# Experts ranked by their tokens on the chip, four of them in 64 places and two passes, with a part of the weights' low parts on GpSimd

## The chip, the cores and the metric

One core of one Trainium2 chip. The metric is the device time of one execution in microseconds, as the median of the runs. Engines: PE (TensorE), DVE (VectorE), ACT (ScalarE), POOL (GpSimd), SP (SyncE, which issues the DMAs).

## What is computed

Two decoder layers over 256 tokens of width 1024, all in fp32. Each has a norm, four token mixers side by side, an output projection, a second norm and a channel mixer: a dense SwiGLU in the first layer, and in the second eight SwiGLU experts of width 3584, of which every token uses two. The part that the change speaks of:

```python
def moe_swiglu(h, router, wg, wu, wd):
    t = h.reshape(-1, D)
    logits = (t @ router).astype(jnp.float32)
    top_vals, top_idx = lax.top_k(logits, TOP_K)
    gates = jax.nn.softmax(top_vals, axis=-1)
    combine = jnp.sum(jax.nn.one_hot(top_idx, N_EXPERTS) * gates[..., None], axis=1)
    y = jnp.zeros(t.shape, jnp.float32)
    for e in range(N_EXPERTS):
        y = y + combine[:, e:e + 1] * swiglu(t, wg[e], wu[e], wd[e])
    return y
```

## The kernel before, in words

All large weights lie in one tensor as chunks of 128 x 2048 floats (1 MB). SP loads them in their order of use into buffers that are taken in turn: `RING` = 9 of them, and `RING2` = 8 more in the MoE stage, in the memory that the mixers have left.

TensorE takes fp32 operands in one pass only with a part of their digits. So every chunk is split, half by half (`halves`, L159 to L178): ACT writes the high part `hi` of 128 x 1024 (L170), DVE the low part `lo` = weight - hi (L171). There are `HALVES` = 4 pairs of such buffers. The other operand is split in the same way by `part` (L206, L207). A product is then three products (`moving`, L188): high by high, low of x by high, high of x by low part of the weights. In the mixers some halves name POOL for the low part (`on_pool`); in the MoE stage none does.

The MoE stage (`moe`) finds the two experts of each token, the place of each token in its expert (`pos`) and the weights (`comb`). `experts` goes through the eight experts in their order. For one of them up to 128 tokens are gathered with a one-hot product (`gather`), transposed and split (`gathered_T`), and stand in TensorE as the stationary operand of 128 columns; the weights move past it, 512 columns at a time. An expert has seven slabs of 512 hidden columns. A slab has six chunks, two each for gate, up and down projection: 24 products for each, 72 in all. `gate_or_up` makes the gate's sum, which ACT puts through silu (L977) into `xs`; DVE multiplies the up sum with it (L981); `act_T` transposes the result (L920), splits it into `hmh` and `hml`; `down` adds it to two banks, and runs one slab behind. At an expert's end `scatter` adds the rows back to `x` with their weights (L955, L956).

If an expert has more than 128 tokens, a second run through all eight takes the places from 128 on (L1000).

The order within each engine's queue is set by the scheduler of the language, not by hand, in the expert loop. Engines work their queues in order. SP's DMAs wait for a free buffer; the gain of the last norm (L125, loaded into `xs`) waits for the last use of `xs` by the last expert's transposes (L892).

The splitting that all stages share:

```python
            eng = nc.gpsimd if j in on_pool else nc.vector
            ...
                nc.scalar.activation(hi, w, AF.Copy)
                eng.tensor_tensor(out=lo, in0=w, in1=hi.bitcast(F32), op=SUB)
```

## Time and profile before

| | us |
|---|---|
| median of 3 runs | 1442.94 |
| lowest and highest | 1442.29 and 1443.75 |
| span of the profiled execution | 1440.7 |
| of it up to the first products of the experts | about 437 |
| PE busy, DVE busy, ACT busy, POOL busy | 1396.5, 1203.5, 981.2, 79.0 |

The times of the runs are those of whole executions. The page gives the profiled execution by its span alone, from the first instruction to the last, and this span is what sums are made against. A busy PE is not PE at its peak: the ends of products are modelled, so a product of 512 columns shows some 394 ns while the next one starts after 229. How far apart products start tells PE's pace.

### The profile page before, as it was taken

What the parts mean: (1) busy time and instruction counts of PE and PEld (TensorE: products, weight loads), DVE (VectorE), ACT (ScalarE), POOL (GpSimd) and SP (SyncE); (2) the same over time, 40 slices, a digit from 0 to 9 for tenths busy, and PEclk for the clock granted to TensorE, in tenths of its full rate; (3) what the DMA queues carried; (4) which work ended last, traced back from release to release, by engine and by line L of the source; (5) the groups of instructions that cost most, each with busy time, mean ns of one, the idle gap of its engine ahead of it and who ended that gap; (6) DMA issues with size and microseconds to landing.
All of it is one profiled execution on the core that took longest, in us unless ns stands there. A gap on an engine that the chain in (4) does not pass through costs nothing.

```text
span 1440.7 us, 19053 instructions
## 1 busy us (share of the span) xinstructions
PE 1396.5 (97%) x6993; PEld 1156.4 (80%) x6994; DVE 1203.5 (84%) x1495; ACT 981.2 (68%) x1223; POOL 79.0 (5%) x46
## 2 busy tenths in 40 slices
PE   8889999998899999999999999999999999999996
PEld 6678999996777888888888888888788888877885
DVE  6986555569968999999998988898898889889886
ACT  5464444453657878788787877777777777777774
POOL 3221000014130000000000000000000000000000
PEclk9999999999999999999999999999999999999998
DMA  9424555553387999999999899999999999919980
GB/s 371 162 111 175 202 181 187 188 211 111 114 353 285 364 373 349 363 370 346 347 362 356 332 362 360 342 368 366 343 350 369 353 350 352 370 67 369 421 333 32
DMA packets 59574, 422.12 MB, mean 293 GB/s; under 512 B 6608, under 2 KB 6864, under 8 KB 9168
## 3 DMA queue, kind: packets, MB, share of 16 engines
q1 hardware_dynamic: 59472, 420.82, 76.9%
q8 instruction: 57, 0.93, 0.3%
q14 instruction: 45, 0.37, 0.1%
HBM read 419.74 MB, written 1.05 MB: 292 GB/s over the span
## 4 chain that ended last, share of the span: by engine, by line
PE 72%; DVE 4%; ACT 1%; issue 0%; POOLq 0%; ACTq 0%; DVEq 0%
PE acc L199 45%; PE sc L199 21%; PE tr L920 2%; DVE cv L381 1%; PE tr L881 1%; DVE lo L171 1%; PE tr L955 1%; PE tr L892 0%; DVE xc L419 0%; ACT hi L170 0%; PE sc L449 0%; DVE raw L856 0%; DVE cv L379 0%; PE tr L243 0%; DVE sel L750 0%
## 5 line engine op out<-in xcount | busy, mean ns | idle before, releaser
L171 DVE TENSOR_TENSOR lo<-raw,hi 128x1024 fp32r<-128x1024 f32 x770 | 916.5, 1228 | 155.4 <-ACT hi L170 132.4
L170 ACT ACTIVATE hi<-raw 128x1024 fp32r<-128x1024 f32 x790 | 803.8, 1056 | 199.2 <-PE acc L199 109.5
L199 PE MATMUL acc<-lo,xgh 128*128 128x512 f32 x896 | 353.0, 394 | 0.7 <-DVE lo L171 0.3
L199 PE MATMUL acc<-hi,xgh 128*128 128x512 f32 x896 | 353.3, 394 | 0.1
L199 PE MATMUL acc<-hi,xgl 128*128 128x512 f32 x896 | 351.2, 392 | 0.0
L199 PEld LDWEIGHTS acc<-lo,xgh 128*128 128x128 f32 x896 | 168.3, 188 | 43.3 <-DVE lo L171 4.4
L199 PEld LDWEIGHTS acc<-hi,xgl 128*128 128x128 f32 x896 | 168.4, 188 | 36.2
L199 PEld LDWEIGHTS acc<-hi,xgh 128*128 128x128 f32 x896 | 168.4, 188 | 34.9 <-ACT xgh L206 0.4
L199 PE MATMUL sc<-hi,hmh 128*128 128x512 f32 x448 | 176.4, 394 | 0.0
L199 PE MATMUL sc<-hi,hml 128*128 128x512 f32 x448 | 175.4, 392 | 0.0
L199 PE MATMUL sc<-lo,hmh 128*128 128x512 f32 x448 | 161.8, 398 | 0.0
L199 PEld LDWEIGHTS sc<-hi,hml 128*128 128x128 f32 x448 | 84.2, 188 | 18.3
L199 PEld LDWEIGHTS sc<-hi,hmh 128*128 128x128 f32 x448 | 84.2, 188 | 18.1
L199 PEld LDWEIGHTS sc<-lo,hmh 128*128 128x128 f32 x448 | 81.9, 188 | 16.3
L199 PE MATMUL sc<-hTh,hi 128*128 128x256 f32 x336 | 93.0, 277 | 0.0
L199 PE MATMUL sc<-hTl,hi 128*128 128x256 f32 x336 | 92.8, 276 | 0.0
L199 PE MATMUL sc<-hTh,lo 128*128 128x256 f32 x336 | 92.8, 276 | 0.0
L206 ACT ACTIVATE hmh<-tr 128x512 fp32r<-128x512 f32 x56 | 33.4, 596 | 68.0 <-PE tr L920 68.0
L199 PE MATMUL acc<-lo,hTh 128*128 128x512 f32 (+1 forms) x192 | 69.4, 388 | 9.2 <-DVE lo L171 9.1
L199 PE MATMUL acc<-hi,hTh 128*128 128x512 f32 (+1 forms) x192 | 70.9, 397 | 0.2
L977 ACT ACTIVATE xs<-acc 128x512 f32<-128x512 f32 x56 | 33.2, 592 | 55.1 <-PE acc L199 55.1
L199 PE MATMUL acc<-hi,hTl 128*128 128x512 f32 (+1 forms) x192 | 70.6, 388 | 0.0
(234 smaller groups left out, 1394.8 us busy)
## 6 DMA issues: line engine op xcount, KB each, us to landing
raw<-wst SPq DMA_DIRECT2D x393, 1024.0 KB, 6.2
raw<-gains SPq DMA_DIRECT2D x4, 512.0 KB, 4.7
raw<-wst SPq DMA_DIRECT2D x4, 512.0 KB, 12.5
pl<-par_l SPq DMA_DIRECT2D x2, 803.5 KB, 9.1
out<-raw SPq DMA_DIRECT2D x4, 256.0 KB, 4.1
x<-x_in SPq DMA_DIRECT2D x2, 256.0 KB, 3.2
x<-x_in SPq DMA_DIRECT2D x1, 512.0 KB, 8.6
xs<-gains SPq DMA_DIRECT2D x1, 512.0 KB, 4.5
```

Of the source, the lines that this page charges most:

```text
L170: nc.scalar.activation(hi, w, AF.Copy)
L171: eng.tensor_tensor(out=lo, in0=w, in1=hi.bitcast(F32), op=SUB)
L199: nc.tensor.matmul(ps, lhs, rhs, start=start and all(m[0] is not ps for m in seq[:n]), stop=stop and all(m[0] is not ps for m in seq[n + 1:]))
L206: a = nc.scalar.activation(hi, src, AF.Copy)
L381: nc.vector.scalar_tensor_tensor(cv[:, ct], src, wk_, cv[:, ct], op0=MUL, op1=ADD)
L881: nc.tensor.matmul(pg[q].rearrange("p k c -> p (k c)"), OH[e][:, t], src[:, t, HF[q]], start=t + n == 0, stop=t + n == 2)
L920: nc.tensor.transpose(ps[:, n], hm[:, n * P:(n + 1) * P], ident)
L955: nc.tensor.matmul(ps, OT[e][:, t], y, start=n == 0, stop=n == 1)
L977: nc.scalar.activation(sg, pg, AF.Silu)
```

## The change

- **Ranking.** `ranks` counts the tokens of each expert and sorts experts 1 to 7 by their number on DVE. SP reads the ranks into registers (L1089 of the changed kernel), and the chunks of all experts but the first are loaded from addresses that depend on them. Expert 0 comes first, then the ranks in the order 3, 0, 4, 1, 5, 2, 6 (`TURNS`).
- **Narrow turns.** The ranks 3 to 6 get 64 places. The high part of their tokens stands in columns 0 to 63 of the stationary operand and the low part in columns 64 to 127 (`both`). Two products then do, with the high and the low part of the weights. The two halves of the rows of a gate's or up projection's sum have to be added: ACT or DVE copies the sum from PSUM to `two` (`folded`, L996 and L998), and one product with a shifted identity (`fold`, L1001) adds the lower rows to the upper ones. Expert 0 and ranks 0 to 2 stay as they are (wide turns).
- **POOL.** In a wide slab 2 of 12 low parts are POOL's, in a narrow one 3 of 12: the second half of the second chunk of gate, up and down projection (`POOLED`).
- **Buffers.** `RING` goes from 9 to 8, `HALVES` from 4 to 5.
- **The second run** is taken when an expert has more tokens than its places.

The comments are left out of the changed file, so lines move: L170, L171 become L182, L183; L977 becomes L1097; L981, L1100; L920, L1028; L199, L211.

```diff
-RING = 9
+RING = 8
-HALVES = 4
+HALVES = 5
+WIDE = 3
+TURNS = (3, 0, 4, 1, 5, 2, 6)
+NARROW = P // 2
+POOLED = ((((), (1,)), ((), (1,)), ((), (1,))), (((), (1,)), ((), ()), ((1,), ())))
...
+            def ranks():
...
+                nc.vector.tensor_add(key, num, cs[:, C_TIE:C_TIE + 8])
+                nc.vector.max(top, key)
+                nc.vector.max_index(ri, top, key)
...
+                def both(hi_lo, ps):
+                    hi = hi_lo[:, :, LO]
+                    nc.scalar.activation(hi, ps[:, :, LO], AF.Copy)
+                    nc.vector.tensor_tensor(out=hi_lo[:, :, UP], in0=ps[:, :, LO], in1=hi.bitcast(F32), op=SUB)
...
+                def rows(items, start, stop):
+                    if len(items[0][1]) == 2:
+                        products([moving(*it) for it in items], start, stop)
+                    else:
+                        products([[(ps, xx[0], w[n])] for n in range(2) for ps, xx, w in items], start, stop)
+                def folded(ps, which, then):
+                    cf = FT[which]
+                    if which == 0:
+                        nc.scalar.activation(cf, ps, AF.Copy)
+                    else:
+                        nc.vector.tensor_copy(cf, ps)
+                    def f():
+                        nc.tensor.matmul(ps, fold, cf, start=False, stop=True, skip_group_check=True)
+                        then()
+                    soon.append(f)
+                def catch_up():
+                    while soon:
+                        soon.pop(0)()
...
-                        hs = w0 if w0 and i + which + j == 0 else halves(c0 + ECH * e + 6 * s + 2 * which + j)
+                        hs = w0 if w0 and i + which + j == 0 else halves(
+                            turns[e].chunk(6 * s + 2 * which + j, False), POOLED[turns[e].wide][which][j])
...
+                        if j == 0:
+                            catch_up()
...
+                    for r in range(NE - 1):
+                        v = nc.values_load(rank_i[0:1, r:r + 1], engines=[mybir.EngineType.SP], min_val=0, max_val=NE - 1)
+                        ranked_c.append(v * ECH + MOE0)
+                    turns = turns + [Turn(ranked_c[r], pos_r, comb_r, r, r < WIDE) for r in TURNS]
...
                     pg = gate_or_up(i, 0)
-                    nc.scalar.activation(sg, pg, AF.Silu)
+                    if narrow:
+                        folded(pg, 0, lambda pg=pg: silu(pg))
+                    else:
+                        silu(pg)
```

How it moves instructions, at two places. ACT in one slab of the expert loop, from one eviction of the transposed activations to the next gate's silu, before. L170 writes high parts of the weights: four of the gate's (raw_8063, raw_8085), two of the up projection's (raw_8118); acc_8062 is the gate's sum.

```order
L206 ACTIVATE hmh_8113<-tr_8108 128x512
L170 ACTIVATE hi_8065<-raw_8063 128x1024
L170 ACTIVATE hi_8069<-raw_8063 128x1024
L170 ACTIVATE hi_8087<-raw_8085 128x1024
L170 ACTIVATE hi_8091<-raw_8085 128x1024
L170 ACTIVATE hi_8120<-raw_8118 128x1024
L170 ACTIVATE hi_8124<-raw_8118 128x1024
L977 ACTIVATE xs_81<-acc_8062 128x512
```

The same engine in a slab of a narrow turn of the changed kernel, from the up projection's first half on (raw_7739 and raw_7759 are its chunks, raw_7778 and raw_7798 the down projection's, acc_7692 the gate's sum):

```order
L182 ACTIVATE hi_7741<-raw_7739 128x1024
L996 ACTIVATE two_7417<-acc_7692 128x512
L182 ACTIVATE hi_7745<-raw_7739 128x1024
L1097 ACTIVATE xs_81<-acc_7692 128x512
L182 ACTIVATE hi_7761<-raw_7759 128x1024
L182 ACTIVATE hi_7765<-raw_7759 128x1024
L182 ACTIVATE hi_7780<-raw_7778 128x1024
L182 ACTIVATE hi_7784<-raw_7778 128x1024
L182 ACTIVATE hi_7800<-raw_7798 128x1024
L182 ACTIVATE hi_7804<-raw_7798 128x1024
L957 ACTIVATE hmh_7859<-tr_7854 128x4x64
L182 ACTIVATE hi_7819<-raw_7817 128x1024
```

The copy of the gate's sum (L996) is new and stands one high part ahead of where the silu stood, so that the up projection's later high parts come behind both.

DVE in one slab before, from the up projection's second half on (L981 multiplies; raw_8118 and raw_8140 are the up projection's chunks, raw_8163 and raw_8185 the down projection's):

```order
L171 TENSOR_TENSOR lo_8125<-raw_8118,hi_8124 128x1024
L171 TENSOR_TENSOR lo_8143<-raw_8140,hi_8142 128x1024
L171 TENSOR_TENSOR lo_8147<-raw_8140,hi_8146 128x1024
L171 TENSOR_TENSOR lo_8166<-raw_8163,hi_8165 128x1024
L981 TENSOR_TENSOR xs_81<-acc_8117,xs_81 128x512
L171 TENSOR_TENSOR lo_8170<-raw_8163,hi_8169 128x1024
L171 TENSOR_TENSOR lo_8188<-raw_8185,hi_8187 128x1024
L171 TENSOR_TENSOR lo_8192<-raw_8185,hi_8191 128x1024
L207 TENSOR_TENSOR hml_8259<-tr_8253,hmh_8258 128x512
```

And in a slab of a narrow turn of the changed kernel, one whole period (acc_7738 is the up projection's sum; raw_7817 and raw_7835 are the next gate's chunks):

```order
L183 TENSOR_TENSOR lo_7742<-raw_7739,hi_7741 128x1024
L183 TENSOR_TENSOR lo_7746<-raw_7739,hi_7745 128x1024
L183 TENSOR_TENSOR lo_7762<-raw_7759,hi_7761 128x1024
L998 CAST two_7417<-acc_7738 128x512
L183 TENSOR_TENSOR lo_7781<-raw_7778,hi_7780 128x1024
L183 TENSOR_TENSOR lo_7785<-raw_7778,hi_7784 128x1024
L1100 TENSOR_TENSOR xs_81<-acc_7738,xs_81 128x512
L183 TENSOR_TENSOR lo_7801<-raw_7798,hi_7800 128x1024
L958 TENSOR_TENSOR hmh_7859<-tr_7854,hmh_7859 128x4x64
L183 TENSOR_TENSOR lo_7820<-raw_7817,hi_7819 128x1024
L183 TENSOR_TENSOR lo_7824<-raw_7817,hi_7823 128x1024
L183 TENSOR_TENSOR lo_7838<-raw_7835,hi_7837 128x1024
```

The low parts of the second halves of raw_7759, raw_7798 and raw_7835 are gone from here; they stand in POOL's queue. The copy of the up sum (L998) comes right behind the first half of the chunk whose second half is POOL's, and two low parts stand between it and the multiplication.

## Rows read from the trace of the kernel before

**Rows 1.** the page, engines: busy us (share of the span) xinstructions

```profile
PE 1396.5 (97%) x6993; PEld 1156.4 (80%) x6994; DVE 1203.5 (84%) x1495; ACT 981.2 (68%) x1223; POOL 79.0 (5%) x46
```

**Rows 2.** windows: PE, PEld, DVE, ACT, POOL busy, PEclk, DMA share, GB/s

```profile
802.00:926.00 124.00, 123.90 (x559) 100.92 (x559) 110.75 (x109) 92.85 (x106) 0.00 (x0) 1.00 0.95 354
1310.00:1390.00 80.00, 78.90 (x353) 64.03 (x353) 71.31 (x69) 59.50 (x66) 0.00 (x0) 1.00 1.01 420
```

**Rows 3.** chain of waits: start us, us, engine, tile, line, xinstructions

```profile
554.95 5.51 PE sc L199 x24
1298.73 5.51 PE sc L199 x24
...
854.71 11.00 PE acc L199 x48
871.65 11.00 PE acc L199 x48
```

**Rows 4.** groups by line, 802 to 926 us: xcount | busy us, mean ns

```profile
L171 DVE TENSOR_TENSOR lo<-raw,hi 128x1024 fp32r<-128x1024 f32 x85 | 98.9, 1220 | 10.0 <-ACT hi L170 10.0
L170 ACT ACTIVATE hi<-raw 128x1024 fp32r<-128x1024 f32 x84 | 82.7, 1052 | 1.6 <-PE acc L199 1.2 <-DVE lo L171 0.3
L199 PE MATMUL acc<-lo,xgh 128*128 128x512 f32 x112 | 44.3, 396 | 0.1
L981 DVE TENSOR_TENSOR xs<-acc,xs 128x512 f32<-128x512 f32 x7 | 4.8, 692 | 3.2 <-PE acc L199 3.2
L920 PE MATMUL tr<-cs,xs 128*128 128x128 f32 x28 | 4.2, 272 | 0.0
L977 ACT ACTIVATE xs<-acc 128x512 f32<-128x512 f32 x7 | 4.2, 598 | 10.0 <-PE acc L199 10.0
L901 ACT ACTIVATE ot<-tr 128x256 fp32r<-128x256 f32 x1 | 0.4, 387 | 1.4 <-PE tr L899 1.4
```

**Rows 5.** timeline of ACT and DVE, one slab: start, us, [idle before]

```profile
860.24 0.60 ACT L977 ACTIVATE xs<-acc 128x512 f32<-128x512 f32 x1 [1.91 <-PE acc L199]
868.47 0.60 ACT L206 ACTIVATE hmh<-tr 128x512 fp32r<-128x512 f32 x1 [1.90 <-PE tr L920]
...
861.81 3.50 DVE L171 TENSOR_TENSOR lo<-raw,hi 128x1024 fp32r<-128x1024 f32 x3 [1.53 <-ACT hi L170]
```

**Rows 6.** timelines of POOL and DVE in the mixers

```profile
401.14 2.39 POOL L171 TENSOR_TENSOR lo<-raw,hi 128x1024 fp32r<-128x1024 f32 x1 [0.26 <-ACT hi L170]
...
401.83 0.48 DVE L617 SCALAR_TENSOR_TENSOR hTl<-tr,gd,hTh 128x256 fp32r<-128x256 f32 x1
402.22 2.38 DVE L171 TENSOR_TENSOR lo<-raw,hi 128x1024 fp32r<-128x1024 f32 x1
...
49.93 3.68 POOL L171 TENSOR_TENSOR lo<-raw,hi 128x1024 fp32r<-128x1024 f32 x1 [5.03 <-ACT hi L170]
...
50.14 1.22 DVE L171 TENSOR_TENSOR lo<-raw,hi 128x1024 fp32r<-128x1024 f32 x1
...
331.35 11.80 POOL L171 TENSOR_TENSOR lo<-raw,hi 128x1024 fp32r<-128x1024 f32 x2 [3.26 <-ACT hi L170]
...
338.26 2.62 DVE L381 SCALAR_TENSOR_TENSOR cv<-zp,pl,cv 128x256 f32<-128x256 f32 x1
```

**Rows 7.** L381 and L171 alone: xcount, min/median/max ns

```profile
L381 DVE SCALAR_TENSOR_TENSOR cv<-zp,pl,cv x120: 468/476/2665, 27.7 to 368.6; 128x256 f32<-128x256 f32 x120
...
L171 POOL TENSOR_TENSOR lo<-raw,hi x20: 2357/2414/9247, 10.5 to 427.6; 128x1024 fp32r<-128x1024 f32 x20
```

**Rows 8.** SP's waits: us in total, times, longest us

```profile
SPq L139 <- DVE lo L171: 919.4, 316, 22.7
SPq L125 <- PE tr L892: 36.2, 1, 36.2
```

**Rows 9.** L999 alone: duration ns min/median/max

```profile
L999 SPq TENSOR_LOAD <-cnti x1: 479/479/479, 1382.5 to 1382.5; - x1
```

**Rows 10.** window at the stage's start, columns as in rows 2

```profile
430.00:440.00 10.00, 7.55 (x32) 5.09 (x33) 7.99 (x29) 4.86 (x8) 0.00 (x0) 0.83 0.52 203
```

More of the change, by code (lines that the diff above doesn't have):

```diff
@@ L57 @@
 C_PLACE = C_IOTA + 8
-C_END = C_PLACE + P
+C_TIE = C_PLACE + P
+C_CAP = C_TIE + 8
+C_END = C_CAP + 8
 Q_RT = 0
@@ new lines, in ranked, with weights @@
+            def ranked(dst, src):
+                t_ = xs[:, 1, :NT * 64].rearrange("p (t r e) -> p t r e", t=NT, r=8)
+                for t in range(NT):
+                    nc.vector.tensor_mul(t_[:, t], by_rank, src[:, t].unsqueeze(1).to_broadcast([P, 8, 8]))
+                nc.vector.tensor_reduce(dst, t_, axis=AX.X, op=ADD)
+            ranks()
+            one_off.close()
+            wk = st.enter_context(tc.tile_pool(name="mw", bufs=1, reuse_waits="tile"))
+            def weights():
@@ L921, in act_T @@
                     hh = wk.tile([P, 4, P], F32R, name="hmh", bufs=2)
-                    hl = wk.tile([P, 4, P], F32R, name="hml", bufs=2)
-                    part(hh, hl, ps)
-                    HT[i] = (hh, hl)
+                    if turns[i // NSLAB].wide:
+                        hl = wk.tile([P, 4, P], F32R, name="hml", bufs=2)
+                        part(hh, hl, ps)
+                        HT[i] = (hh, hl)
+                    else:
+                        both(hh, ps)
+                        HT[i] = (hh,)
                 def down(i, between=()):
@@ L930, in down @@
                     for j in range(2):
-                        hs = halves(c0 + ECH * e + 6 * s + 4 + j)
+                        hs = halves(turns[e].chunk(6 * s + 4 + j, i == NE * NSLAB - 1 and j == 1), POOLED[turns[e].wide][2][j])
                         order = [(n, hf) for n in range(2) for hf in range(2)]
@@ L935, in down @@
                             order.sort(key=lambda o: o[1])
-                        products([moving(DP[e][hf], cut(HT[i], ALL, 2 * j + n), cut(hs[n], ALL, HF[hf])) for n, hf in order],
-                                 s + j == 0, s == NSLAB - 1 and j == 1)
+                        rows([(DP[e][hf], cut(HT[i], ALL, 2 * j + n), cut(hs[n], ALL, HF[hf])) for n, hf in order],
+                             s + j == 0, s == NSLAB - 1 and j == 1)
+                        if j == 0:
+                            catch_up()
                         for f in between if j == 0 else ():
@@ L971, in experts, with silu, mul @@
                 one_hot_T(0)
-                if place is pos:
+                if oh is not None:
                     weights()
+                    for r in range(NE - 1):
+                        v = nc.values_load(rank_i[0:1, r:r + 1], engines=[mybir.EngineType.SP], min_val=0, max_val=NE - 1)
+                        ranked_c.append(v * ECH + MOE0)
+                    turns = turns + [Turn(ranked_c[r], pos_r, comb_r, r, r < WIDE) for r in TURNS]
                 for i in range(NE * NSLAB):
                     e, s = divmod(i, NSLAB)
+                    narrow = not turns[e].wide
+                    def silu(pg):
+                        nc.scalar.activation(sg, pg, AF.Silu)
+                    def mul(pu):
+                        nc.vector.tensor_mul(hm, pu, sg)
                     pg = gate_or_up(i, 0)
-                    nc.scalar.activation(sg, pg, AF.Silu)
+                    if narrow:
+                        folded(pg, 0, lambda pg=pg: silu(pg))
+                    else:
+                        silu(pg)
                     if s:
@@ L980, in experts @@
                     pu = gate_or_up(i, 1)
-                    nc.vector.tensor_mul(hm, pu, sg)
+                    if narrow:
+                        folded(pu, 1, lambda pu=pu: mul(pu))
+                    else:
+                        mul(pu)
                     if s == NSLAB - 1 and e + 1 < NE:
                         gather(e + 1)
+                        catch_up()
                     if s:
@@ L995, in experts @@
                 finish(adds, raw().rearrange("p (t d) -> p t d", t=NT))
-            experts(pos, oh, w0)
-            most = nc.values_load(cnti[0:1, 0:1], min_val=0, max_val=S)
-            with tc.If(most > P):
+            ranked_c = []
+            experts([Turn(MOE0, pos, comb, 0, True)], oh, w0)
+            most = nc.values_load(cnti[0:1, 0:1], min_val=0, max_val=2 * S)
+            with tc.If(most > S):
                 pos2 = mo.tile([P, NT, 8], F32, name="pos2")
-                nc.vector.tensor_scalar(pos2, pos, float(P), None, op0=SUB)
-                experts(pos2)
+                off = mo.tile([P, 8], F32, name="off")
+                nc.vector.tensor_reduce(off, by_rank[:, WIDE:NE - 1].rearrange("p r e -> p e r"), axis=AX.X, op=ADD)
+                nc.vector.tensor_scalar(off, off, float(NARROW - P), float(P), op0=MUL, op1=ADD)
+                for t in range(NT):
+                    nc.vector.tensor_sub(pos2[:, t], pos[:, t], off)
+                experts([Turn(MOE0 + e * ECH, pos2, comb, e, True) for e in range(NE)])
     done = mixer(0, 0, None)
```

94 lines of the change are left out of this document (69 added, 25 removed).

## The prediction

> **What bounds the kernel now.** I first read the busy shares of the page: PE is busy for 97% of the span, DVE for 84%, POOL for 5% [rows 1]. Then the stretches: over the expert of 802 to 926 us PE is busy for 99.9% of the time at a granted clock of 1.00 (its level of 2.4 GHz), DVE for 89%, ACT for 75%, POOL not at all [rows 2]. The weights look like a second limit there, since the 16 DMA engines show a share of 0.95 at 354 GB/s; but from 1310 to 1390 us, where the queue catches up, the same engines move 420 GB/s [rows 2]. Six chunks of 1.049 MB, which is what a slab needs, take 15.0 us at that rate, and DMA is not the limit. The chain of waits shows the period. The first products of two experts lie at 554.95 and 1298.73 us, six experts apart: 124.0 us for an expert. Two slabs of one expert start at 854.71 and 871.65 us: 16.94 us for a slab, of which 48 products take 11.00 us, so 0.229 us each [rows 3]. Seven slabs make 118.6 us; the other 5.4 us are the change of expert (gather, transposes). So the MoE stage is PE's, eight times 124.0 us, and the other engines wait for it inside their queues: ACT stands idle for 1.91 us ahead of the silu (L977) and 1.90 us ahead of the eviction hmh, DVE for 1.53 us until a high part comes [rows 5].
>
> **The change, part by part.** All sums go against the profiled execution, 1440.7 us; the median of the runs lies 2.2 us above it.
>
> *Fewer passes.* Of the 504 weight products of a narrow expert 168 go and 14 folds come: 154 times 0.229 us is 35.3 us less of PE. It is a gain only if nothing else then needs more than 16.94 us for a slab. DMA needs 15.0 us. ACT has twelve high parts at 0.985 us (82.7 us by 84) and three smaller operations: 13.4 us [rows 4]. That would be about 2 us less than now in each of the 28 narrow slabs.
>
> *The ring of waits in a narrow slab.* The engines work their queues in order, and the new order closes a ring. ACT's first eviction of the gate (L996) waits for the gate's last product. After it stand one high part, the silu (L1097) and the two high parts of the up projection's second chunk; the low part of the last one is POOL's; PE must use it before DVE can copy the up result (L998); after that copy DVE has two low parts in front of the multiplication (L1100); then come four transposes and ACT's eviction (L957); and only behind this the four high parts of the next gate stand, the last of which has its low part on POOL again. Priced by rows [rows 4, 7]:
>
> - eviction 0.60, high part 0.985, silu 0.60, two high parts 0.985 + 1.05: 4.22 us
> - POOL's low part, 2.36 us, and PE's last two products, 0.23 + 0.39 = 0.62 us
> - DVE's copy, not in the trace, at the price of the other 512-column operations on PSUM, 0.69 us
> - two low parts at 1.164 us (98.9 by 85), the multiplication 0.69: 3.02 us
> - transposes 0.60 us, eviction of 256 elements 0.39 us
> - four high parts 4.00 us, POOL 2.36 us, PE 0.62 us
>
> The sum is 18.9 us, more than PE's 16.94. Priced the same way, the ring of before has neither copies nor POOL in it: silu, three high parts, a low part, the multiplication, transposes, eviction, four high parts, a low part and the last products make 12.6 us. It fits into 16.94, as the idle times of ACT say [rows 5].
>
> *POOL against DVE.* Nothing in the MoE stage of before shows them together, so I go by the mixers. At 401.14 us POOL starts a low part of 2.39 us; DVE's own low part, issued at 402.22, takes 2.38 us instead of 1.22 and ends 1.07 us behind POOL's. From 49.93 us POOL needs 3.68 us because it first waits for a low part of DVE that ends at 51.36. An L381 that takes 0.476 us in the median takes 2.62 us at 338.26, when POOL is in: 2.14 us lost [rows 6, 7]. Operations that read PSUM go on (L617, 0.48 us at 401.83 inside POOL's span). So a low part moved to POOL saves DVE 1.16 us and can cost it 2.14 us. In a narrow slab nine on DVE, three on POOL and the three operations on PSUM are 10.5 + 6.4 + 1.8 = 18.7 us: the pair is as full as the ring is long. Two of POOL's three low parts are in the ring already. The third, of the down projection's second chunk, becomes ready about 8 us into the ring, while DVE does the two low parts ahead of the multiplication. If it gets in between them, the ring grows by 2.14 us to 21.0; if DVE finishes first, it stays at 18.9.
>
> The rows show both orders: POOL got in behind a single low part at 51.36 us, and waited out a chain of L381 from 331.35 us on, where its two low parts took 11.80 us [rows 6]. The Trainium skill ("SBUF — State Buffer", Who interferes with whom) says that whichever of the two issues first holds the shared port for its whole instruction. By that rule POOL would always enter after one low part, and the slab would take 21.0 us; by the row at 331.35 it would take 18.9. The Trainium skill ("Perfetto Trace Analysis", GPSIMD Engine Instruction) calls GpSimd's spans in a profile unreliable; with the 2.14 us that DVE lost in place of POOL's 2.36, twice, the ring would be 0.4 us shorter.
>
> I take the middle, 20.0 us: 3.06 us more than now. 28 such slabs: +86 us (+55 to +114).
>
> *Change of expert in a narrow turn.* At 5.4 us it is PE's now; PE is idle for some 8 us of a 20 us slab and can do part of it there. I take half off, 4 times 2.7 us: -11 us (-22 to 0).
>
> *Wide turns.* 84 x 3 products as before. DVE and POOL need ten low parts, two of POOL's and two operations on PSUM, 11.6 + 4.3 + 1.4 = 17.3 us if nothing overlaps, against PE's 16.94. The operations on PSUM don't wait for POOL, so most of it fits: +4 us over 28 slabs (0 to +8).
>
> *Ranks.* Some sixteen DVE operations of 0.1 to 0.2 us and two for the fold stand among the first low parts, where PE waits: the stretch from 430 to 440 us already has PE at 7.55 of 10 us and a granted clock of 0.83 [rows 10]. +3 us (0 to +6). SP's seven register loads, at 0.48 us (L999) 3.4 us together, stand behind the twelve chunks that SP has issued ahead, some 34 us of PE's work at 2.8 us each: hidden [rows 9].
>
> *A buffer less.* SP waits 919 us in all for a buffer to come free [rows 8], so it runs as far ahead as buffers allow. Sixteen buffers are 45 us of PE's work instead of 48. The longest hold is the gain of the last norm, 36.2 us in which SP issues nothing else [rows 8]. It still fits: +1 us (0 to +3).
>
> *Sum:* 86 - 11 + 4 + 3 + 1 = +83, which is 1523.7 us for the execution and **1526 us** for the median. The bounds are 55 - 22 = +33 and 114 + 8 + 6 + 3 = +131: 1476 to 1574 us, the forecast's own range.
>
> **Rivals.**
>
> *The narrow slabs run at the speed of DMA.* The ring opens if ACT and POOL run ahead in the five pairs of buffers and POOL does not hold DVE up. Then a narrow slab takes 15.0 us, 28 x -1.94 = -54; with -11 and +8 from above the median is 1386 us. It decides from where a slab falls under 16.94 us. For it: PE, ACT and DMA each have the room. Against it: ACT's queue has the gate's eviction ahead of the up projection's high parts, and in every case of [rows 6] in which both engines read two SBUF operands one of the two stood still.
>
> *Only the port counts.* If the waits fill each other and just the serial work on the shared port is left, 9 x 1.164 + 3 x 2.14 = 16.9 us, a slab is what it was: 0 - 11 + 8 gives a median of 1440 us, no change within what can be told.
>
> *The clock falls.* With PE busy for 12 of 20 us, its level may drop to 1.2 GHz for a while, as it did between 430 and 440 us [rows 10]. PE's three steps in the ring, 0.62 + 0.60 + 0.62 us, would double: at most 28 x 1.84 = +51 us, a median of 1577 us.
>
> *The change falls back.* With more than 64 tokens for one of the last four experts the whole stage runs a second time, about +990 us. The reference's routing gives 62, 66, 94, 33, 86, 63, 56 and 52 tokens; the fourth of the ranked seven has 63, so it takes two flips by rounding.
>
> **How the numbers follow.** The forecast gets 0.62, DMA's speed 0.15, the port alone 0.12 (half of it over 0.2% faster, half within), the clock 0.10, the second pass 0.01. About 0.2% is what a measurement of this kernel can tell from no change. Faster is 0.15 + 0.06 = 0.21, within 0.06, slower 0.73. A range of 1425 to 1580 us takes in the forecast's own, the port alone and the clock, and leaves out DMA's speed, the second pass and a few tails, together 0.2.
>
> **What would show it.** In the changed profile: narrow slabs of 19 to 21 us beside wide ones of 17; low parts of DVE (L183) of over 2 us wherever one of POOL lies beside them; ACT idle ahead of L957 and L996, DVE ahead of L998; DMA's share well under 0.9 in the narrow turns. I am wrong if narrow slabs take under 17 us, if DVE's low parts stay at 1.22 us beside POOL, or if the wide slabs grow by over 0.5 us.

## The result, and the profile after

The changed kernel takes 1632.6 us (median of four runs, 1630.7 to 1635.2), the kernel before 1442.6 us on the same chip: a ratio of 1.132, with an interval of 1.130 to 1.134. Slower was right; 83 us were forecast and 190 came, well outside the range. The profiled execution spans 1633.7 us against 1440.7, so 193.0 us have to be found.

The page of the changed kernel, engines, as in [rows 1]:

```profile
PE 1402.1 (86%) x6378; PEld 1047.7 (64%) x6378; DVE 1229.8 (75%) x1402; ACT 969.7 (59%) x1251; POOL 441.1 (27%) x186
```

PE has 615 instructions fewer and is busy for longer; no engine but PE is above 75%. The windows, columns as in [rows 2], of a wide turn, a narrow turn, one wide slab and one narrow slab:

```profile
732.00:868.00 136.00, 130.51 (x561) 99.93 (x560) 113.34 (x97) 92.92 (x107) 38.09 (x14) 1.00 0.88 328
868.00:1032.00 164.00, 122.33 (x406) 75.80 (x406) 114.78 (x94) 92.26 (x111) 52.77 (x21) 0.91 0.74 267
802.40:821.10 18.70, 18.20 (x80) 13.87 (x79) 15.55 (x13) 12.96 (x16) 4.98 (x2) 1.00 0.91 338
908.10:931.40 23.30, 16.72 (x55) 10.05 (x54) 16.25 (x12) 12.83 (x16) 7.58 (x3) 0.93 0.72 268
```

A narrow slab takes 23.3 us, a wide one 18.7, both 16.94 before. In neither does an engine work for the whole time, and DMA's share falls to 0.74. In the narrow turn the mean granted clock is 0.91. From the starts of the silu, which mark the slabs, the 193.0 us come out as follows: the first silu at 461.3 us instead of 446.6, +14.7; the first turn (wide) +1.8; the other three wide turns 136.0 us instead of 124.1, +35.6 together; the four narrow ones 149.1, 163.6, 162.5 and 167.5 us instead of 123.4, 124.1, 124.2 and 130.0, +141. The first narrow turn is the shortest because its second and third slab take 16.0 and 17.1 us, with all three of GpSimd's low parts in them:

```profile
599.80:615.80 16.00, 13.88 (x58) 9.82 (x57) 15.64 (x13) 13.16 (x15) 7.80 (x3) 1.00 0.84 324
```

The order there is another one: one low part of DVE, not two, stands between the copy (L998) and the multiplication (L1100). From the fourth slab on, this turn is like the other narrow ones.

The groups by line of the narrow turn from 868 to 1032 us, columns as in [rows 4], show who is waited for:

```profile
L183 DVE TENSOR_TENSOR lo<-raw,hi 128x1024 fp32r<-128x1024 f32 x63 | 99.7, 1606 | 16.3 <-ACT hi L182 16.1
L183 POOL TENSOR_TENSOR lo<-raw,hi 128x1024 fp32r<-128x1024 f32 x21 | 52.8, 2513 | 112.4 <-ACT hi L182 87.4 <-PE acc L211 19.5 <-PE sc L211 5.5
L211 PE MATMUL acc<-lo,xgh 128*128 128x512 f32 x110 | 40.2, 441 | 22.2 <-POOL lo L183 13.4 <-DVE lo L183 8.7
L211 PE MATMUL sc<-lo,hmh 128*128 128x512 f32 x56 | 22.6, 514 | 15.5 <-DVE lo L183 12.9 <-POOL lo L183 2.6
```

DVE makes 63 low parts instead of 85 and is busy with them for 99.7 us instead of 98.9: what GpSimd took over saved DVE nothing. PE waits 37.7 us for low parts.

One narrow slab, from one eviction (L957) to the next, in the timelines of ACT, DVE, POOL and PE (start, duration, [idle time before, and what ended it]):

```profile
1244.77 0.39 ACT L957 ACTIVATE hmh<-tr 128x256 fp32r<-128x256 f32 x1 [6.96 <-PE tr L1028]
1245.05 4.85 ACT L182 ACTIVATE hi<-raw 128x1024 fp32r<-128x1024 f32 x5
1252.67 0.60 ACT L996 ACTIVATE two<-acc 128x512 fp32r<-128x512 f32 x1 [2.78 <-PE acc L211]
1253.17 1.05 ACT L182 ACTIVATE hi<-raw 128x1024 fp32r<-128x1024 f32 x1
1254.12 0.59 ACT L1097 ACTIVATE xs<-acc 128x512 f32<-128x512 f32 x1
1254.59 5.80 ACT L182 ACTIVATE hi<-raw 128x1024 fp32r<-128x1024 f32 x6
1267.84 0.39 ACT L957 ACTIVATE hmh<-tr 128x256 fp32r<-128x256 f32 x1 [7.45 <-PE tr L1028]
...
1249.93 3.01 DVE L183 TENSOR_TENSOR lo<-raw,hi 128x1024 fp32r<-128x1024 f32 x1 [0.30 <-ACT hi L182]
...
1259.97 0.69 DVE L998 CAST two<-acc 128x512 fp32r<-128x512 f32 x1 [3.06 <-PE acc L211]
1260.58 4.51 DVE L183 TENSOR_TENSOR lo<-raw,hi 128x1024 fp32r<-128x1024 f32 x2
1265.02 0.68 DVE L1100 TENSOR_TENSOR xs<-acc,xs 128x512 f32<-128x512 f32 x1
...
1249.07 2.78 POOL L183 TENSOR_TENSOR lo<-raw,hi 128x1024 fp32r<-128x1024 f32 x1 [8.77 <-ACT hi L182]
1256.73 2.42 POOL L183 TENSOR_TENSOR lo<-raw,hi 128x1024 fp32r<-128x1024 f32 x1 [4.88 <-PE acc L211]
1260.52 2.35 POOL L183 TENSOR_TENSOR lo<-raw,hi 128x1024 fp32r<-128x1024 f32 x1 [1.37 <-PE sc L211]
...
1264.01 2.36 PE L211 MATMUL sc<-lo,hmh 128*128 128x512 f32 x4 [2.33 <-DVE lo L183]
1266.17 1.05 PE L211 MATMUL sc<-hi,hmh 128*128 128x512 f32 x2
1267.02 0.78 PE L1028 MATMUL tr<-cs,xs 128*128 128x128 f32 x4
```

The ring of the prediction can be followed from row to row; these differences of starts add up to the whole 23.07 us:

| step | forecast | measured |
|---|---|---|
| eviction (L957), four high parts | 0.39 + 4.00 | 4.30 |
| GpSimd's low part of the gate | 2.36 | 2.78 |
| PE's last products of the gate | 0.62 | 0.82 |
| gate's copy (L996), a high part | 1.59 | 1.45 |
| silu (L1097), two high parts | 2.63 | 2.61 |
| GpSimd's low part of the up projection | 2.36 | 2.42 |
| PE's last products of it | 0.62 | 0.82 |
| DVE's copy (L998) | 0.69 | 0.61 |
| two low parts | 2.33 | 4.44 |
| multiplication (L1100) | 0.69 | 0.68 |
| until the transposes are evicted | 0.60 | 2.14 |
| sum | 18.9 | 23.07 |

Two rows carry the difference: DVE's two low parts, during which GpSimd holds one of its own from 1260.52 on, and the way from the multiplication's end at 1265.70 to the eviction at 1267.84. For the latter the windows show the clock; columns as in [rows 2]:

```profile
1260.50:1264.00 3.50, 0.96 (x3) 0.48 (x3) 3.50 (x3) 0.00 (x0) 2.35 (x1) 1.00 0.75 283
1264.00:1267.40 3.40, 3.39 (x8) 2.27 (x9) 2.83 (x3) 0.00 (x0) 0.00 (x0) 0.50 0.49 116
```

PE was busy for 0.96 of 3.50 us, since it waited for the low part that DVE could not make; then the granted clock is 0.50, the level of 1.2 GHz, for as long as the products ahead of the transposes last. Five slabs of this turn have such a stretch, at 1195.7, 1219.6, 1243.5, 1264.0 and 1287.9 us.

### The profile page after: what moved, and what is told of

Its sections match the earlier page's. It is cut to its first block, busy times and chain, and to the rows that moved or that the text cites. A ratio compares the mean times of both kernels' runs of the same rounds, so it can differ in the third digit from the quotient of the medians.

```text
span 1633.7 us, 18506 instructions
## 1 busy us (share of the span) xinstructions
PE 1402.1 (86%) x6378; PEld 1047.7 (64%) x6378; DVE 1229.8 (75%) x1402; ACT 969.7 (59%) x1251; POOL 441.1 (27%) x186
## 3 DMA queue, kind: packets, MB, share of 16 engines
q1 hardware_dynamic: 59472, 420.82, 68.6%
## 5 line engine op out<-in xcount | busy, mean ns | idle before, releaser
L183 DVE TENSOR_TENSOR lo<-raw,hi 128x1024 fp32r<-128x1024 f32 x630 | 922.1, 1496 | 179.4 <-ACT hi L182 175.4
L182 ACT ACTIVATE hi<-raw 128x1024 fp32r<-128x1024 f32 x790 | 787.8, 1054 | 151.6 <-PE acc L211 61.7
L183 POOL TENSOR_TENSOR lo<-raw,hi 128x1024 fp32r<-128x1024 f32 x160 | 424.1, 2652 | 911.4 <-ACT hi L182 779.0
L211 PE MATMUL acc<-lo,xgh 128*128 128x512 f32 x896 | 341.6, 422 | 102.3 <-POOL lo L183 52.4
L211 PE MATMUL acc<-hi,xgh 128*128 128x512 f32 x896 | 326.4, 406 | 0.9 <-ACT hi L182 0.8
L211 PEld LDWEIGHTS acc<-lo,xgh 128*128 128x128 f32 x896 | 158.5, 191 | 207.6 <-DVE lo L183 103.0
L211 PE MATMUL sc<-lo,hmh 128*128 128x512 f32 x448 | 169.6, 446 | 61.2 <-DVE lo L183 51.8
L211 PEld LDWEIGHTS acc<-hi,xgh 128*128 128x128 f32 x896 | 168.2, 191 | 52.4 <-ACT hi L182 17.6
L211 PE MATMUL acc<-hi,xgl 128*128 128x512 f32 x448 | 177.3, 396 | 0.0
L211 PE MATMUL sc<-hi,hmh 128*128 128x512 f32 x448 | 174.1, 435 | 0.6 <-ACT hi L182 0.6
L211 PEld LDWEIGHTS sc<-lo,hmh 128*128 128x128 f32 x448 | 85.9, 206 | 106.4 <-DVE lo L183 73.6
L957 ACT ACTIVATE hmh<-tr 128x256 fp32r<-128x256 f32 x28 | 10.8, 385 | 180.2 <-PE tr L1028 180.2
L211 PEld LDWEIGHTS sc<-hi,hmh 128*128 128x128 f32 x448 | 90.6, 208 | 19.5 <-ACT hi L182 3.2
L211 PEld LDWEIGHTS acc<-hi,xgl 128*128 128x128 f32 x448 | 84.6, 189 | 19.1
L211 PE MATMUL sc<-hTh,hi 128*128 128x256 f32 x336 | 93.0, 277 | 0.0
L211 PE MATMUL sc<-hTl,hi 128*128 128x256 f32 x336 | 92.9, 277 | 0.0
L211 PE MATMUL sc<-hTh,lo 128*128 128x256 f32 x336 | 92.9, 276 | 0.0
L211 PE MATMUL sc<-hi,hml 128*128 128x512 f32 x224 | 88.4, 395 | 0.0
L998 DVE CAST two<-acc 128x512 fp32r<-128x512 f32 x28 | 19.3, 691 | 78.9 <-PE acc L211 78.9
L211 PE MATMUL acc<-lo,hTh 128*128 128x512 f32 (+1 forms) x192 | 70.0, 391 | 7.1 <-DVE lo L183 7.1
L211 PE MATMUL acc<-hi,hTh 128*128 128x512 f32 (+1 forms) x192 | 72.5, 407 | 0.1
L211 PE MATMUL acc<-hi,hTl 128*128 128x512 f32 (+1 forms) x192 | 71.4, 392 | 0.0
```

The costliest lines, as they stand in the source:

```text
L211: nc.tensor.matmul(ps, lhs, rhs, start=start and all(m[0] is not ps for m in seq[:n]), stop=stop and all(m[0] is not ps for m in seq[n + 1:]))
L957: nc.scalar.activation(hi, ps[:, :, LO], AF.Copy)
L998: nc.vector.tensor_copy(cf, ps)
```

## The experiments

Ratios are to the kernel before, on the same chip, with their 95% interval.

### GpSimd taken out, wholly and by kind of turn

```diff
-POOLED = ((((), (1,)), ((), (1,)), ((), (1,))), (((), (1,)), ((), ()), ((1,), ())))
+POOLED = ((((), ()), ((), ()), ((), ())), (((), ()), ((), ()), ((), ())))              # e1
+POOLED = ((((), ()), ((), ()), ((), ())), (((), (1,)), ((), ()), ((1,), ())))          # e2
+POOLED = ((((), (1,)), ((), (1,)), ((), (1,))), (((), ()), ((), ()), ((), ())))        # e3
```

> Edit: the changed kernel with every low part of the MoE on DVE; ranks, narrow turns, 8 chunk buffers and five pairs of halves stay. Theory A (GpSimd's low parts are what made the ring long: 2.4 to 2.8 us instead of 1.2 each, the two ahead of the multiplication held up, and TensorE idle so long that its clock halves): the ring of a narrow slab is 0.60 + 0.985 + 0.60 + 2.03 + 1.20 + 0.62 + 0.69 + 2.33 + 0.69 + 0.60 + 0.39 + 4.00 + 1.20 + 0.62 = 16.6 us, a wide slab is 16.95 again, and what is left is the 14.7 us by which the first silu came late: about 1458 us (1440 to 1480). Theory B (the ring is long by its waits in order, the two copies, the folds and the halved clock, whoever makes the low parts): narrow slabs stay over 20 us and only the wide ones get back their 1.7 us, 21 x 1.7 = 36: about 1590 us.

> Edit: GpSimd makes low parts in the wide turns only (two of twelve in a slab); the narrow turns have all on DVE. Theory A: the kernel without GpSimd's low parts plus what they cost in the wide slabs, 18.65 - 16.95 = 1.7 us in 21 slabs and 0.2 in seven: +37 us, about 1495 us. Theory B: in a wide slab the same number of low parts moved costs nothing and the 1.7 us come from the narrow neighbours (late transfers): about the time without GpSimd, within 10 us.

> Edit: GpSimd makes low parts in the narrow turns only (three of twelve in a slab); the wide turns have all on DVE. Theory A: narrow slabs of 23 us as in the changed kernel, wide ones of 16.95: 1633 - 37 = about 1596 us, some 140 us above the kernel without GpSimd's low parts. Theory B: the narrow slabs are as long without GpSimd, so this and the kernel without it differ by under 20 us.

Measured: 1464.7 us (1.016, 1.014 to 1.018), 1491.7 us (1.036, 1.034 to 1.038) and 1607.7 us (1.116, 1.114 to 1.118). All three lie within 12 us of theory A, and the two parts add up: 27.0 + 143.0 + 1464.7 is 1634.7, the change 1632.6. So 168 of the 190 us hang on GpSimd's low parts, 143 of them in the narrow turns. Without them a narrow slab takes 17.72 us, not 16.6; its window (columns as in [rows 2]):

```profile
1107.70:1125.40 17.70, 15.27 (x55) 8.77 (x54) 15.42 (x15) 12.81 (x16) 0.00 (x0) 1.00 0.93 352
```

The clock stays at 1.00, but no engine works through: it is still the ring, now 0.8 us longer than PE's 16.94.

In a wide slab of the later turns GpSimd costs 1.45 us (18.62 in e2, 17.17 in e1). PE works through such a slab in e1; in the changed kernel it stands ahead of low parts. POOL and DVE of one wide slab of the changed kernel:

```profile
807.18 2.53 POOL L183 TENSOR_TENSOR lo<-raw,hi 128x1024 fp32r<-128x1024 f32 x1 [6.12 <-ACT hi L182]
817.32 2.45 POOL L183 TENSOR_TENSOR lo<-raw,hi 128x1024 fp32r<-128x1024 f32 x1 [7.60 <-ACT hi L182]
...
808.55 3.39 DVE L183 TENSOR_TENSOR lo<-raw,hi 128x1024 fp32r<-128x1024 f32 x2
...
818.17 3.81 DVE L183 TENSOR_TENSOR lo<-raw,hi 128x1024 fp32r<-128x1024 f32 x2 [0.67 <-ACT hi L182]
```

Both times DVE's two low parts take 3.4 and 3.8 us instead of 2.4, and PE's product with GpSimd's low part of the gate starts 0.54 us after its predecessor, at 819.82, instead of 0.23; what the gaps of that slab over 0.30 us have above 0.23 adds up to 1.4 us.

The first turn is wide too, and GpSimd makes the same two low parts in each of its slabs, but there they cost nothing: 17.17 us with them (the changed kernel and e2) and without (e1). A window and two rows of the first turn, and a row of a later wide one:

```profile
488.00:505.20 17.20, 17.20 (x78) 13.99 (x77) 15.10 (x13) 13.65 (x16) 5.05 (x2) 1.00 1.01 419
508.47 3.46 DVE L183 TENSOR_TENSOR lo<-raw,hi 128x1024 fp32r<-128x1024 f32 x2 [1.27 <-ACT hi L182]
501.35 1.07 ACT L182 ACTIVATE hi<-raw 128x1024 fp32r<-128x1024 f32 x1 [0.33 <-PE acc L211]
...
802.37 0.60 ACT L1097 ACTIVATE xs<-acc 128x512 f32<-128x512 f32 x1 [2.36 <-PE acc L211]
```

DVE's pair is held up in the first turn as well (3.46 us), and yet PE is busy for all of the slab. There ACT is so far ahead that it waits for PE to give a buffer of halves back; in the later turns it stands 2.0 to 2.4 us ahead of the silu and makes the next high parts only then. That this reserve makes the difference is argued from these rows; no run changes it alone.

### The third low part of a narrow slab

```diff
-POOLED = ((((), (1,)), ((), (1,)), ((), (1,))), ...
+POOLED = ((((), (1,)), ((), (1,)), ((), ())), ...
```

> Edit: the changed kernel, but in the narrow turns the third of GpSimd's low parts (the down projection's second chunk) goes back to DVE, behind the multiplication; the gate's and the up projection's stay on GpSimd. Theory A (that low part always gets in between DVE's two low parts ahead of the multiplication and adds 2.1 us to the ring): narrow slabs of 21 us instead of 23.2, 24 to 28 of them by 2.1 us: 50 to 60 us less than the change, about 1577 us. Theory B (it runs where DVE would wait anyway, the excess is the clock's and that of the other two low parts): a DVE with ten low parts instead of nine is no faster, 1620 to 1640 us.

Measured: 1564.0 us (1.084, 1.082 to 1.086), 68.6 us less than the change. Theory A has the right term and too small a size: narrow slabs take 19.90 us, 3.3 less. DVE and ACT of one of them:

```profile
1181.22 2.35 DVE L183 TENSOR_TENSOR lo<-raw,hi 128x1024 fp32r<-128x1024 f32 x2
1183.49 0.68 DVE L1100 TENSOR_TENSOR xs<-acc,xs 128x512 f32<-128x512 f32 x1
...
1185.30 0.39 ACT L957 ACTIVATE hmh<-tr 128x256 fp32r<-128x256 f32 x1 [4.28 <-PE tr L1028]
```

The two low parts take 2.27 us again instead of 4.44, and from the multiplication's end (1184.17) to the eviction it is 1.13 us instead of 2.14. The second difference is the clock: it is 1.00 throughout this slab.

### The clock by itself

Products that nothing reads, where TensorE waits:

```diff
-                        products([[(ps, xx[0], w[n])] for n in range(2) for ps, xx, w in items], start, stop)
+                        hi_lo = [[(ps, xx[0], w[n])] for n in range(2) for ps, xx, w in items]
+                        products(hi_lo[:len(items)], start)
+                        if fill:
+                            busy(fill, cs[:, :64].bitcast(BF16), cs[:, :256].bitcast(BF16))
+                        products(hi_lo[len(items):], False, stop)
...
```

> Edit: the changed kernel with 18 products that nothing reads added to each narrow slab, where TensorE waits for the low parts of the gate, of the up projection's second chunk and of the down projection's first one; the queues of the other engines keep their order. Theory A (the clock's fall to its lower level, once in each narrow slab, costs the 1.5 us by which the transposes come late): the granted clock of a narrow turn is 1.00 instead of 0.91 to 0.94, slabs of about 21.7 us, 24 to 28 times 1.5: about 1594 us. Theory B (the clock falls where TensorE has time anyway): the clock is 1.00, and the time stays or grows by the products that stand in the way, 1632 to 1650 us.

Measured: 1606.1 us (1.114, 1.112 to 1.116), 26.5 us less. Between the two: the added products kept the clock in some slabs and not in others, which gives the price slab by slab. Windows of three following slabs of one turn:

```profile
884.30:907.60 23.30, 19.13 (x74) 11.77 (x73) 16.24 (x12) 12.85 (x17) 7.58 (x3) 0.93 0.75 269
907.60:930.30 22.70, 19.08 (x74) 11.72 (x73) 16.24 (x12) 12.80 (x17) 7.58 (x3) 0.92 0.74 278
930.30:952.30 22.00, 17.77 (x76) 10.68 (x74) 15.97 (x12) 13.04 (x17) 7.30 (x3) 1.00 0.78 284
```

At a clock of 1.00 the slab takes 22.0 us, with a fall in it 22.7 to 23.3: the clock costs 0.7 to 1.3 us of a slab. In the slab at 1.00 it is 1.12 us from the multiplication's end (941.86) to the eviction (942.98), against 2.14 in the changed kernel, with the same 4.51 us for DVE's pair. The total is no clean measure of the clock: in the first narrow turn the scheduler found another order, in which slabs took 17.9 us with all three of GpSimd's low parts in them:

```profile
631.80:649.70 17.90, 16.54 (x73) 11.19 (x73) 17.90 (x13) 13.29 (x16) 8.60 (x3) 1.00 0.93 351
```

DVE is busy there for the whole slab, with nine low parts and the three operations on PSUM. So 17.9 us is what the shared port and DVE's own work come to, with no wait of the ring left in it.

### Buffers, ranks, and the place of the buffers

```diff
-RING = 9              # kernel before
-HALVES = 4
+RING = 8              # e4: 8 and 5;  e14: 8 and 4
+HALVES = 5
```

> Edit: the kernel before with 8 chunk buffers instead of 9 and five pairs of halves instead of four, nothing else. Theory A (the 12.2 us by which the last stage of the second mixer came later than before, ahead of any rank, are the chunk buffer's): about 1455 us, with the first silu 12 us later than at 446.6 us and slabs of 16.95 us behind it. Theory B (they come from the larger table of constants and from another order that the scheduler found): 1443 to 1446 us, and the first silu at 447 to 449 us.

> Edit: the kernel before with 8 chunk buffers instead of 9, four pairs of halves as before. Theory A (the chunk buffer is what the mixers miss): first silu about 12 us later than at 446.6 us, about 1452 us, as with 8 buffers and five pairs. Theory B (the fifth pair changed the order in the mixers and lost the time there): first silu at 447 to 450 us, about 1443 us.

Measured: 1452.5 us (1.007, 1.006 to 1.009) and 1443.0 us (1.001, 1.000 to 1.002). With 8 buffers and five pairs the first silu comes at 459.9 us; with 8 and four it comes at 447.1, and nothing that can be told is lost. So theory A of e4 had the right time from the wrong cause: with 8 buffers, it is the fifth pair of halves. With 8 and four, the queues of ACT, DVE and GpSimd up to the first silu hold the same operations in the same order as before; with 8 and five ACT's differs in some 20 places, from 27 us on. In the trace of e4 the loss stands in the mixers, +4.8 us by the first silu of the dense layer (140.4 us) and +12.1 us by 437.5; the DMA share from 100 to 140 us is 0.35 instead of 0.42. Which of these places loses the time was not followed further.

```diff
-WIDE = 3              # e6, without GpSimd's low parts
+WIDE = 7
...
```

```diff
-C_END = C_PLACE + P   # e13, kernel before
+C_END = C_PLACE + P + 16
```

> Edit: the kernel without GpSimd's low parts, with all seven ranked experts in 128 places and three passes; ranks, register loads and transfers by a register stay, and 8 chunk buffers with five pairs of halves. Theory A (ranks cost what they add ahead of the first products, 450.2 - 446.6 = 3.6 us, and the buffers 10.3): 1442.2 + 13.9 = about 1456 us, wide slabs of 16.95 us. Theory B (the 17.17 us that wide slabs take in every kernel with ranks so far, the first expert's too, belong to the new code as such): 0.23 us in 49 to 56 slabs more, about 1468 us.

> Edit: the kernel before with 16 columns more in the table of constants, which nothing reads: all later buffers lie 64 bytes further, every engine's queue is the same. Theory A (TensorE's products follow each other at 0.233 instead of 0.229 us because of where the buffers lie): slabs of 17.17 us, 56 times 0.23: about 1455 us. Theory B (the place of the buffers does nothing, the 0.23 us belong to something else in the new code): 1441 to 1444 us, slabs of 16.94 us.

Measured: 1466.7 us (1.017, 1.015 to 1.019) and 1442.3 us (1.001, 1.000 to 1.002). Theory B of e6: wide slabs take 17.17 us with the new code even where nothing is narrow and GpSimd makes nothing. The same 72 products follow each other at 0.233 us on average instead of 0.230. Where the buffers lie, at least by these 64 bytes, is not the cause (e13); the cause stays open.

### The ring opened

First the second copy goes to ACT (e8, without GpSimd's low parts), then also 9 buffers and four pairs (e9):

```diff
-                    if which == 0:
-                        nc.scalar.activation(cf, ps, AF.Copy)
-                    else:
-                        nc.vector.tensor_copy(cf, ps)
+                    nc.scalar.activation(cf, ps, AF.Copy)
```

> Edit: the kernel without GpSimd's low parts, with the copy of the up result for the fold on ACT instead of DVE. Theory A (what is left is the ring, 17.72 us measured for it, in which DVE's copy waits for TensorE with two low parts and the multiplication behind it): without the 0.69 us of the copy and the 0.6 us of TensorE's last products in it a narrow slab takes about 16.4 us, 28 times 1.3 less: about 1430 us. Theory B (DVE's or DMA's load sets 17.72, or another wait takes over): 1455 to 1475 us.

> Edit: the same with 9 chunk buffers and four pairs of halves, as in the kernel before. Theory A (the fifth pair is not needed for the ring, and the buffer given up for it costs 10 us ahead of the MoE): 10 us less than the same kernel with 8 and five, about 1420 us. Theory B (in a narrow slab ACT needs the fifth pair to run ahead): the 10 us come back at the start and are lost again in narrow slabs, longer by 0.5 us or more.

Measured: 1450.7 us (1.006, 1.004 to 1.007) and 1443.5 us (1.001, 1.000 to 1.002). Theory A of e8 fails in size: a narrow slab takes 17.17 us, 0.55 less instead of 1.3. Only the copy itself has left DVE's queue. Its waits in e8 (L1097 is the multiplication there),

```profile
1099.12 1.23 DVE L183 TENSOR_TENSOR lo<-raw,hi 128x1024 fp32r<-128x1024 f32 x1 [1.26 <-ACT hi L182]
1100.56 3.50 DVE L183 TENSOR_TENSOR lo<-raw,hi 128x1024 fp32r<-128x1024 f32 x3 [0.21 <-ACT hi L182]
1104.93 0.69 DVE L1097 TENSOR_TENSOR xs<-acc,xs 128x512 f32<-128x512 f32 x1 [0.88 <-PE acc L998]
```

are as long as in e1: 1.26 and 0.21 us for ACT's high parts behind the gate's copy and the silu, and 0.82 us there for PE. e9 gains 7.3 us, where theory A said 10: the first silu comes at 450.2 instead of 457.7 us, and the slabs are the same.

Then the order itself, in the five middle slabs of each narrow turn:

```diff
+                    hs = halves(c(6 * s + 2, False))
+                    folded(pg, 0, lambda: None)
+                    some(pu, hs, 0, 0)
+                    catch_up()
+                    some(pu, hs, 0, 1)
...
+                    hs = halves(c(6 * s + 3, False), (), lambda: silu(pg))
...
+                    hs = halves(c(6 * s - 2, False))
+                    folded(pu, 1, lambda: None)
...
+                    mul(pu)
```

> Edit: the kernel without GpSimd's low parts and with both copies on ACT, and in the five middle slabs of each narrow turn the order of ACT, DVE and TensorE is written by hand: ACT makes two high parts of the up projection ahead of the gate's copy and one more ahead of the silu, the copy of the up result stands behind two high parts of the down projection, DVE's multiplication behind two low parts more, the evictions behind the next gate's first low parts. Theory A (the order closed the ring; open, a slab takes what DVE has to do, 12 x 1.164 + 0.69 + 0.42 = 15.1 us, near DMA's 15.0): 17 to 20 slabs by 1.8 us less than the same kernel in the scheduler's order, about 1418 us. Theory B (another wait or DMA, whose share is 0.94 at 17.17 us, sets the slab): 1440 to 1452 us.

> Edit: the same with 9 chunk buffers and four pairs of halves. Theory A (buffers buy 7 us ahead of the MoE as with the scheduler's order, and the order by hand does without the fifth pair): about 1411 us. Theory B (with four pairs ACT can't get as far ahead as the order by hand asks): narrow slabs of 16 us and more, 1420 to 1435 us.

> Edit: the narrow slabs in the order by hand, with 9 chunk buffers and four pairs of halves, and the multiplication of a turn's first slab ahead of its transposes. Theory A (a narrow slab is DVE's 15.1 us once the ring is open): as the run before it in this order, about 1424 us, middle slabs of 15.1 us, 1.2% under the kernel before. Theory B (the early transposes of the first slab were part of that time): 4 slabs by 1 to 2 us more, 1428 to 1432 us.

Measured: 1435.5 us (0.994, 0.992 to 0.996), 1424.3 us (0.987, 0.986 to 0.989) and 1434.9 us (0.996, 0.994 to 0.997). In e10 and e11 the transposes of a narrow turn's first slab read what the expert before left there, so these two kernels compute something else, and their totals only show what the order of the other slabs is worth; e12 puts that slab's multiplication ahead. In all three the middle slabs take 15.07 us, as theory A had it; the totals of e10 and e11 missed theirs by 17 and 13 us, mostly because the first slab that the hand order takes over stayed at 18.2 us. Waiting for the first multiplication cost another 10 us in e12 (theory B, and more than it said).

```diff
                     hs = halves(c(6 * s, False))
                     catch_up()
-                    act_T(i - 1)
+                    if s > 1:
+                        act_T(i - 1)
                     some(pg, hs, 0, 0)
                     some(pg, hs, 0, 1)
                     hs = halves(c(6 * s + 1, False))
+                    if s == 1:
+                        act_T(i - 1)
...
```

> Edit: the order by hand, with the transposes of a turn's first slab behind both chunks of the next gate instead of between them, and the additions to x of the expert before at two later places. Theory A (TensorE waited 2.3 us there for the multiplication, and DVE 2.5 and 1.3 us for products that stood behind TensorE's waits): first and second slab of a narrow turn shorter by 5 us together, 4 times 5: about 1415 us. Theory B (the first slab is bound by the hand-over from the scheduler's order): 1430 to 1436 us.

Measured: 1419.6 us (0.984, 0.983 to 0.986): the fastest of all, 22 us under the kernel before. Theory A is near (about 1415 us): the first slab of the hand order falls from 18.5 to 16.4 us. The longest stop of DVE in one middle slab, and that slab's window (columns as in [rows 2]):

```profile
856.88 3.50 DVE L183 TENSOR_TENSOR lo<-raw,hi 128x1024 fp32r<-128x1024 f32 x3 [0.20 <-ACT hi L182]
```

```profile
855.30:870.40 15.10, 14.24 (x56) 8.82 (x54) 14.75 (x15) 13.34 (x18) 0.00 (x0) 1.00 1.01 421
```

DVE has one stop of 0.20 us, and DMA's share is 1.01 at 421 GB/s: the narrow slab now stands at two limits at once, DVE's work (15.1 us by theory A of e10) and DMA's 15.0 us, and the runs don't part them.

Last, the same order with GpSimd's three low parts:

> Edit: the run before it in this order, with three low parts of each narrow slab on GpSimd as in the change (the gate's, the up projection's and the down projection's second chunks, second halves). Theory A (the port alone: while GpSimd holds it DVE stands still, so DVE and GpSimd take 9 x 1.164 + 3 x 2.14 + 1.1 = 18 us one after the other, also with the ring open): narrow middle slabs of 18 us and more instead of 15.1, 20 times 3: about 60 us more than the run before it. Theory B (only the ring made GpSimd dear): DVE is freed of 3.5 us a slab, DMA's 15.0 us is the limit, and the time is that of the run before it or a few us less.

Measured: 1528.8 us (1.060, 1.059 to 1.062), 109 us more. Middle slabs take 18.4 to 20.2 us. Theory B is out; theory A has the sign, and its 60 us were too few. Windows of two of these slabs:

```profile
895.90:916.10 20.20, 15.10 (x55) 10.14 (x55) 16.64 (x12) 13.65 (x17) 8.35 (x3) 0.92 0.84 314
916.10:934.50 18.40, 14.29 (x58) 9.15 (x57) 14.96 (x11) 13.74 (x18) 8.50 (x3) 1.00 0.78 297
```

From 898.4 to 918.6 us DVE's nine low parts take 15.6 us, alone twelve would take 14.0: DVE loses more than it was relieved of, also with this order. The slab of 18.4 us, at a clock of 1.00, is near theory A's 18; the one of 20.2 has a fall of the clock in it and waits of ACT for PE of 1.4 and 4.6 us, in an order that was not written for GpSimd.

## Why the prediction was wrong

Of the 193.0 us, 83 were forecast. The 110 that are missing lie in three places: the narrow turns (+141 instead of 86 - 11 = +75), the wide turns (+37 instead of +4), and what stands ahead of the first silu (+14.7 instead of 3 + 1 = +4).

*What bounded the kernel, fewer passes.* Right: PE's work in a narrow slab fell (15.27 us busy in e1), and DMA has the room (15.07 us a slab in e15).

*The ring.* Right as a mechanism and in its path, step for step as the table shows. The forecast of 20.0 us for a slab was 3.2 us short. Of the 23.2 us that most narrow slabs of the three later turns take, 17.7 are there without GpSimd (e1), 2.2 come with its first two low parts (19.9, e5), 2.1 with the third (22.0, e7), and up to 1.3 with the clock.

*POOL against DVE.* The step that failed first: between 18.9 and 21.0 us I took the middle. The third low part is not an even chance. It becomes ready by PE's work (1260.52) just ahead of the end of DVE's copy (1260.66), so in 19 of the 28 narrow slabs it starts 0.06 to 0.12 us ahead of DVE's two low parts, and not between them. The first of the two then takes 3.38 us,

```profile
1260.58 3.38 DVE L183 TENSOR_TENSOR lo<-raw,hi 128x1024 fp32r<-128x1024 f32 x1
```

the second 1.21, and the pair 4.51, which is 2.27 + 2.24. The Trainium skill ("SBUF — State Buffer", Who interferes with whom) says that the first to issue holds the port for its instruction; the trace agrees, with GpSimd 0.06 us ahead and the 3.38 us. So 21.0 us was the right end. Taking a mean of two cases that don't both occur was the mistake. The ring without the third low part was another 1.0 us longer than 18.9 (19.9 in e5): PE's last products twice 0.2 us, GpSimd waiting 0.45 us for a low part of DVE, and 0.5 us in which the transposes stand behind two products.

*The clock.* It was a rival with a chance of 0.10 and at most 1.84 us a slab. It came on top of the forecast rather than in its place: up to 1.3 us in most narrow slabs, and by the same low part of GpSimd: it holds up DVE's, for which PE waits until 1264.01. The two should not have been exclusive cases: a longer ring means more idle time on PE.

*Wide turns.* +4 us forecast, +37 measured: 18.7 us a slab in the later turns, 1.7 more than before, where the prediction itself called over 0.5 a sign that it is wrong. I counted work against 16.94 us and found that it fits. It does in the first turn, where ACT is ahead; in the other three a low part that takes 2.4 instead of 1.2 us, or stands behind such a one, comes late, and PE loses 1.4 us in such a slab. A wait that I had at nothing, because the busy times left room for it, was the cost. Besides, 0.23 us a slab belong to the new code (e6).

*Change of expert.* Roughly right: turns of 163.6 us with slabs of 23.2 leave 1.2 us for it, where 5.4 were and 2.7 were forecast; this is a difference, not a stretch that was read by itself.

*Ranks.* Right: with 9 buffers and four pairs the first silu comes at 450.2 us (e9), 3.6 us late, against +3.

*A buffer less.* +1 forecast, +1.0 measured (e14), which can't be told from nothing (1.000 to 1.002). SP's longest wait is not the gain's 36.2 us but one of 47.1 (L857, for the output); it stands behind the last chunk and holds nothing up. But the change also made a fifth pair of halves, and that edit I did not cost at all: 10 us (e4).

*Rivals.* A narrow slab comes to DMA's 15.0 us (15.07 in e15), but only once the order is open and GpSimd is out, and DVE's work ends at the same time. The port alone was priced at 16.9 us, without the three operations on PSUM (1.8 us) that the prediction counts in its own 18.7; with DVE busy for a whole slab it took 17.9 us (first narrow turn of e7), and 18.4 to 20.2 in e16. So it did speak against the change, not for no difference.

## What to carry to other kernels

Work given to an engine that shares a port with the one it relieves has to be costed as a stop of the other, and a low part on the way of a loop of waits by its own, longer time; a count of busy time hides both. Whether the stop then shows in the total seems a question of reserve: the same two low parts cost nothing in the first wide turn and 1.45 us a slab in the later ones. Where passes are taken from the engine that bounds, write down the order of the other queues as a ring before trusting the saving: here the saving of 154 products per expert was only to be had (1419.6 instead of 1632.6 us) with the relief undone, both copies on ACT, the old buffers and three engines' order written by hand. Cost every constant that a change touches, also one that looks like mere room.

## What the runs showed that I had not expected

- A fifth pair of buffers for the halves costs 10 us (1452.5 against 1443.0 us) ahead of the stage that it was made for. The queues' order in the mixers changes with it.
- The same 72 products of a wide slab take 17.17 instead of 16.94 us in every kernel with the new code; the place of the buffers, 64 bytes further, changes nothing, and the cause is open.
- The granted clock falls to 0.50 for 3.4 us within the running stage, once in most narrow slabs, after 3.5 us in which PE was busy for 0.96 us; its price is not the slower products as such, but that the transposes, which ACT waits for, stand behind them (2.14 us instead of 1.13 in e5 and 1.12 in e7).
